# Larger recurrence steps, and TensorE in written order, in the first stage of a hybrid decoder layer

## The chip, the cores and the metric

The kernel runs on one core of one Trainium2 chip. Its time is the device time of one execution in microseconds (us); a run of a kernel is summarised by the median of its executions. Profiles come from one profiled execution.

Five engines work side by side, each through its own instructions in order: TensorE (PE in the profile; its weight loads are PEld), VectorE (DVE), ScalarE (ACT), GpSimd (POOL) and SyncE (SP), which here issues nearly all DMA transfers. They wait for each other by semaphores.

## What is computed

One layer on 2048 tokens of width 1024, all in float32:

```
h = RMSNorm(x)
[hgrn2 columns | rwkv7 columns] = h @ W_in           # 2048 + 1792 columns
o_hgrn2 = HGRN2 recurrence, 4 heads of 128           # S_t = diag(f_t) S_{t-1} + k_t v_t^T
o_rwkv7 = RWKV-7 recurrence, 8 heads of 64           # S_t = S_{t-1} diag(w_t) + (S_{t-1} a_t) b_t^T + v_t k_t^T
x = x + concat(o_hgrn2, o_rwkv7) @ W_out
x = x + ConvFFN(RMSNorm(x))                          # up, causal conv w=3, SiLU gate, down; d_ff 2816
out = RMSNorm(x)
```

## The kernel before

**Stages.** `phase1` (stage 1) computes the input projection, both recurrences and the output projection of three of the four token blocks of 512. Stage 2 does the last output projection, the up-projection, the convolution and gate, and the down-projection. The change is in stage 1 alone.

**Matmuls in three.** A projection in float32 is made of three matmuls on operands split in a high and a low part (`mm3`, lines 258 to 261): `hh*wh`, `hl*wh`, `hh*wl`. The weights are loaded as `wraw`, cast to `wh` on ACT (line 243) and subtracted to `wl` on DVE (line 244).

**Three streams.** Stage 1 is written as three Python generators, whose instructions are emitted in turn:

- `dense()` yields after each `mm3`, with a cost in ns (648 in a projection, 680 in an output projection). It goes through all projection columns, evicts each accumulator into `rkv`, `hq`, `hf`, `hv`, `hgg` and so on, transposes (`turn`, `transposed`) and runs `out_block`.
- `rw_super(nb, s_)` computes RWKV-7 for one block and two pairs of heads, a superblock; there are eight, one after the other.
- `hg_unit(nb, j)` computes HGRN2 for one block and one head; there are sixteen.

A loop at the end of `phase1` takes one step of `rw_super` (to its next `yield`), one of `hg_unit`, and then as many `mm3` of `dense` as make up `TICK` ns:

```python
        while any(alive.values()):
            for key, g in (("r", rw_), ("h", hg_)):
                ...
            fill(TICK)
```

With costs of 770 us in all, `TICK` 2000 gives about 386 rounds. The order so written is a priority: the Tile framework's scheduler, which works when the program is built, then puts each engine's instructions into an order of its own, in which an instruction that it expects to wait is passed by others. At run time each engine takes its instructions strictly in the built order.

**A superblock, in order.** Line numbers are those of before.

1. `ai`: two pairs of matmuls with the decay and gate LoRA weights (627, 629), sigmoids, a scan on DVE (637), exponentials; `W` is set to 1 in a column (643).
2. Norms through matmuls with `blk1` (648, 666); products `RT`, `AT`, `KB`, `BV` on DVE (649 to 676).
3. `M`: 64x128 matmuls (687), masked by DVE multiplies (690).
4. The 32x32 diagonal blocks of `M` go to DRAM (`Ed`, 703) and come back with one block per partition (`E`, 705).
5. Transposes `KBT`, `AT`, `v` (711 to 725), `lv` (742).
6. `Ti`, set to the identity (750, 751), becomes the inverse in 31 row steps of a multiply and an add on DVE (757, 759), with a yield after every fourth.
7. `Ti` and its transposed copy `TiT` (764) go to DRAM (`Td`, 763, 765) and come back as `TZ` (775) and `TTs` (772).
8. `z` (786), `z2` (800), `qu` (814), `yg` (834), `xp` and `yp` (850, 857) are small matmuls, each followed by an eviction.
9. `ch`: eight serial steps (868), each with a DVE multiply; then `yp` (878), a norm (886), the gate `gm` (898) and the output.

**A unit of HGRN2.** `scaled(l)` makes four DVE multiplies per level (927 to 932) for seven levels on `q`, `k`, `f` and `Sf`, which starts as ones (920). The levels' matmuls are at 948, transposes at 990, the state at 1001 and the output at 1010 and 1011.

Pool buffers of DRAM, SBUF and PSUM are few in stage 1: two PSUM banks for projections (`pj`), two for HGRN2 (`hg`), two double banks for RWKV-7 (`rw`), and four `wraw`.

Of the kernel before, what the change touches and what calls it, by code (L numbers as in the profile page):

```python
# [7 lines left out]
F32 = mybir.dt.float32  # L8
# [3 lines left out]
AF = mybir.ActivationFunctionType  # L12
# [6 lines left out]
P = 128  # L19
# [4 lines left out]
NBLK = T // BLK  # L24
FF = 2816
NFF = FF // P
TICK = 2000.0
NEG_C = -0.6065306597126334
HG_SCALE = 128.0 ** -0.5

# [31 lines left out]
def tile_layer(ctx, tc, consts, x, norm1_w, w_in, hg_lb_logits, hg_norm_w, rw_shift_mu, rw_w0, rw_w2,  # L62
# [3 lines left out]
    nc = tc.nc  # L66
    V, S, TE = nc.vector, nc.scalar, nc.tensor
# [41 lines left out]
    def act(out_, in_, func, **kw):  # L109

        want = tables.get(func)
        if want is not None and want != tab["now"]:
            pre = S.preload_act_table_set(want)
            for u_ in tab["uses"]:
                tc.add_manual_dep(pre.ins, u_.ins.name, NOSYNC, reason="table order")
            tab.update(now=want, pre=pre, uses=[])
        i_ = S.activation(out_, in_, func, **kw)
        if want is not None:
            tc.add_manual_dep(i_.ins, tab["pre"].ins.name, NOSYNC, reason="table order")
            tab["uses"].append(i_)  # L120
        return i_
# [141 lines left out]
    def phase1(c1):  # L263
# [3 lines left out]
        rp = c1.enter_context(tc.tile_pool(name="rp", bufs=1, reuse_waits="tile"))  # L267
# [342 lines left out]
        def rw_super(nb, s_):  # L610
# [6 lines left out]
            def tile_(tag, shape, name):  # L617
                return rp.tile([P] + shape, F32, tag=tag, name=name)

            def bank2():  # L620
                return ps.tile([P, 2, BLK], F32, tag="rw", name="rw", bufs=2)

            ai = tile_("KBT", [2, 2, BLK], "ai")
            a, iW = ai[:, 0], ai[:, 1]
# [5 lines left out]
            for u in U:  # L630
                act(a[:, u], bs_[u][:, 0, :], AF.Sigmoid, bias=vec("a0", prs[u]))
                act(iW[:, u], bs_[u][:, 1, :], AF.Sigmoid, bias=vec("w0", prs[u]))
            yield
            mk_ = tile_("M", [4, 2, BLK], "mk")
            c, km, sq = mk_[:, 0], mk_[:, 1], mk_[:, 2]
            for u in U:
                V.tensor_tensor_scan(c[:, u], scanm, iW[:, u], 0.0, ALU.mult, ALU.add)
                act(sq[:, u], k[:, u], AF.Square, scale=vec("kk", prs[u]))
                act(km[:, u], a[:, u], AF.Identity, bias=oka[:, prs[u]:prs[u] + 1], scale=vec("ka", prs[u]))
            yield  # L640
            W = tile_("UV", [16, 65], "W")
            WC = tile_("WC", [16, 1], "WC")
            V.memset(W[:, :, 0:1], 1.0)
            act(W[:, :, 1:65], c16(c), AF.Exp, scale=NEG_C)
            act(iW, c, AF.Exp, scale=-NEG_C)
            b1 = bank2()
            for u in U:
                TE.matmul(b1[:, u, :], blk1, sq[:, u], start=True, stop=True)
            V.tensor_scalar_max(sq, b1, 1e-24)
            V.tensor_mul(km, km, k)  # L650
            yield
            act(sq, sq, AF.Ln)
            act(sq, sq, AF.Exp, scale=-0.5)
            V.tensor_copy(WC, W[:, :, 64:65])
# [11 lines left out]
                TE.matmul(b1[:, u, :], blk1, BV[:, u], start=True, stop=True)  # L666
            for u in U:
                V.scalar_tensor_tensor(c[:, u], k[:, u], vec("kk", prs[u]), sq[:, u], ALU.mult, ALU.mult)
            yield
            V.scalar_tensor_tensor(AT, r4(c), -1.0, W4[:, :, :, 0:64], ALU.mult, ALU.mult)  # L670
            KB = tile_("KB", [8, 4, 64], "KB")
            V.tensor_mul(KB[:, :, 0::3, :], v16(km), v16(iW))
            yield
            V.tensor_mul(a, a, iW)
            V.tensor_mul(KB[:, :, 1:3, :], v16(c), v16(a))
            V.tensor_mul(BV, b1, v)
# [3 lines left out]
            for j in range(2):  # L680
                for u in U:
                    s1 = bank2()
                    for i in range(4):
                        b, e = 2 * j + i // 2, i % 2
                        for h in range(2):
                            hr = slice(h * 64, h * 64 + 64)
                            TE.matmul(s1[:, h, i * P:i * P + P], KB[hr, 4 * u + b, 2 * e:2 * e + 2, :],
                                      AR[hr, u, :, 2 * b + e, :], start=True, stop=True)
                    for h in range(2):
                        V.tensor_mul(M[:, u, :, 2 * j:2 * j + 2, h, :].rearrange("p e b t -> p b e t"),  # L690
                                     s1[:, h].rearrange("p (b e t) -> p b e t", e=2, t=P),
                                     s1m.unsqueeze(1).unsqueeze(1).broadcast_to([P, 2, 2, P]))
                    yield

            E = rp.tile([P, 32, 32], F32, tag="E", name="E")
            Ed = dp.tile([64, 32, 32], F32, tag="Ed", name="Ed", bufs=2)
# [7 lines left out]
                            M[r0:r0 + 32, u, e, :, :, 32 * q:32 * q + 32].rearrange("p b h t -> p (b h) t"))  # L704
            dma(E[0:64], Ed)

            KBT = tile_("KBT", [2, 8, P], "KBT")
            for u in U:
                tp = bank2()
# [19 lines left out]
            act(RHS[64:128, :, :, 0:64], tpv[0:64], AF.Copy)  # L729
            act(RHS[0:64, :, :, 0:64], tpv[64:128], AF.Copy)  # L730
            done["rw1"] += 1
            yield

            lv = bank2()
            for u in U:
                for b in range(4):
                    for h in range(2):
                        for e in range(2):
# [4 lines left out]
                                      UV[kr:kr + 64, 4 * u + b, e, h * 64:h * 64 + 64], start=True, stop=True,  # L743
                                      tile_position=(kr, r0))
            act(RHS[:, :, :, 64:128], lv.rearrange("p u (b h t) -> p (u b) h t", h=2, t=64), AF.Copy)
            yield

            n = 64
            Ti = rp.tile([P, 32, 32], F32, tag="Ti", name="Ti")
            V.memset(Ti[0:n], 0.0)  # L750
            V.memset(Ti[0:n].rearrange("m a b -> m (a b)")[:, 0:1024:33], 1.0)
            yield
            for j in range(31):
                nr, ncol = 31 - j, j + 1
                tmp = rp.tile([P, 272], F32, tag="etmp", name="etmp")
                tv = tmp[0:n, 0:nr * ncol].rearrange("m (a b) -> m a b", b=ncol)
                V.tensor_mul(tv, E[0:n, j, j + 1:32].unsqueeze(2).broadcast_to([n, nr, ncol]),
                             Ti[0:n, j, 0:ncol].unsqueeze(1).broadcast_to([n, nr, ncol]))
                V.tensor_add(Ti[0:n, j + 1:32, 0:ncol], Ti[0:n, j + 1:32, 0:ncol], tv)
                if j % 4 == 3:  # L760
                    yield
            TiT = rp.tile([P, 32, 32], F32, tag="E", name="TiT")
            dma(Td[0], Ti[0:n])
            V.tensor_copy(TiT[0:n], Ti[0:n].rearrange("m a b -> m b a"))
            dma(Td[1], TiT[0:n])
            TZ = tile_("XH", [2, 2, 4, 2, 32], "TZ")
            for u in U:
                for e in range(2):
                    r0 = er0(e)
                    for q in range(2):  # L770
# [3 lines left out]
                    m0 = u * 32 + e * 16  # L774
                    dma(TZ[r0:r0 + 32, 0, u].rearrange("p b h t -> p (b h) t"),
                        Td[0, m0:m0 + 8].rearrange("m s t -> s m t"))
            for _ in range(2):
                yield
            z = bank2()
            for u in U:  # L780
                for b in range(4):
# [64 lines left out]
            for u in U:  # L846
                for ch in range(8):
                    b, e = ch // 2, ch % 2
# [4 lines left out]
            for u in U:  # L853
                for ch in range(8):
                    b, e = ch // 2, ch % 2
# [6 lines left out]
            for ch in range(8):  # L862
                b, e = ch // 2, ch % 2
# [42 lines left out]
        def hg_unit(nb, j):  # L906
# [6 lines left out]
            for b in range(4):  # L913
                TE.transpose(tp[:, b * P:(b + 1) * P], v[:, b * P:(b + 1) * P], ident)
            act(VT, tp.rearrange("p (b t) -> p b t", t=P), AF.Copy)
            yield
            A = rp.tile([P, 4, 64], F32, tag="hA", name="A")
            Pf = f
            Sf = rp.tile([P, BLK], F32, tag="Sf", name="Sf")
            V.memset(Sf, 1.0)  # L920

            def scaled(l):

# [34 lines left out]
            Xs = []  # L958
            for l in range(3):
                Xs.append(scaled(l))  # L960
                yield
            l0, l1 = bank("hg"), bank("hg")
            level(l0, 0, k, q)
            for l in range(3):
# [1 line left out]
            V.tensor_mul(A, l0[:, 0:256].rearrange("p (b t) -> p b t", t=64), dgm.unsqueeze(1).broadcast_to([P, 4, 64]))  # L966
            for l in range(3):
                take(l, l1, l * 128)
            yield
            Xs = []  # L970
            for l in range(3, 6):
                Xs.append(scaled(l))
                yield
            l1 = bank("hg")
            for l in range(3, 6):
                level(l1, (l - 3) * 128, Xs[l - 3], Xs[l - 3], l)
# [1 line left out]
                take(l, l1, (l - 3) * 128)  # L978
            act(Af[0:64, :, 0:64], A[0:64], AF.Copy)
            act(Af[64:128, :, 64:128], A[64:128], AF.Copy)  # L980
            yield
            X = scaled(6)
            V.tensor_mul(k, k, Sf)
            V.tensor_mul(q, q, Pf)
# [71 lines left out]
        while any(alive.values()):  # L1056
            for key, g in (("r", rw_), ("h", hg_)):
                if alive[key]:
                    try:
                        next(g)  # L1060
                    except StopIteration:
                        alive[key] = False
            fill(TICK)


    if "1" in stages:
        with ExitStack() as c1:
            phase1(c1)
    cx.close()

# [13 lines left out]
    with ExitStack() as c2:  # L1084
# [35 lines left out]
        with tc.tile_pool(name="op", bufs=1, reuse_waits="tile") as op_:  # L1120
# [4 lines left out]
            b = NBLK - 1  # L1125
# [363 lines left out]
```

## Time and profile before

| | |
|---|---|
| median of 3 runs | 2780.48 us (2779.83 to 2783.94) |
| span of the profiled execution | 2783.2 us |
| last projection matmul of stage 1 starts | 1416.33 us |
| first matmul of stage 2 starts | 1425.53 us |
| input-projection matmuls into `pj`, three lines of 960 | 401.8 + 379.9 + 379.0 us busy |
| DMA | 435.01 MB, mean 156 GB/s |

A row of a timeline reads: start in us, duration, engine, line, operation, output<-inputs, shapes, count, and in brackets the idle time before it with what ended it. "SPq" is a DMA issue on SP. A row of a group of instructions ends with their busy time in us and the mean in ns, then the idle time before them. A row of waits reads: engine, output and line, what it waited for, total us, times, longest. A row of windows gives the stretch, its length, then for PE, PEld, DVE, ACT and POOL the busy us with the number of instructions, then the granted share of the TensorE clock, the share of the DMA engines and GB/s; "sum" adds up the stretches asked for. A matmul's duration includes its way through the array; matmuls overlap, so the distance from start to start is what one occupies.

### The profile page before, as it was taken

The page shows a single profiled execution, that of the slowest core. Times are in us where ns is not written, and L with a number is a line of the kernel's source. Part 1 is how long each engine was busy: PE and PEld are TensorE (multiplying, and loading weights), DVE is VectorE, ACT ScalarE, POOL GpSimd, SP SyncE. Part 2 cuts the span into 40 slices and gives each one's busy share as a digit, 9 for nine tenths or more (in the row PEclk, how much of TensorE's full clock was granted, in tenths as well). Part 3 has the DMA queues.
Part 4 walks back from the last instruction along what each step waited for, and adds up shares of the span by engine and source line. Part 5 has one row for each costly group of instructions (what it writes and reads, how often), then busy time and mean ns, then how long its engine had stood idle before and what let it go on. Part 6 is the DMA issues. An engine that isn't in the chain of part 4 may idle for free.

```text
span 2783.2 us, 47784 instructions
## 1 busy us (share of the span) xinstructions
PE 2678.8 (96%) x18059; PEld 2135.2 (77%) x18059; DVE 2066.4 (74%) x3877; ACT 1421.1 (51%) x2254; POOL 11.1 (0%) x24
## 2 busy tenths in 40 slices
PE   8999999989999999999989999998999999999998
PEld 6877777767787777777767888886888888877887
DVE  4867778685686766868658789989997877677656
ACT  5445454544646446435346765456455555445444
POOL 0000000000000000000000000000000000000000
PEclk9999999999999999999899999999999999999999
DMA  5222322244441344543475457756672223998855
GB/s 163 72 69 72 99 73 78 63 131 141 131 121 58 102 141 136 161 132 94 131 239 178 143 172 262 239 165 216 205 245 88 87 76 135 324 333 310 289 193 186
DMA packets 429628, 435.01 MB, mean 156 GB/s; under 512 B 68703, under 2 KB 288213, under 8 KB 429397
## 3 DMA queue, kind: packets, MB, share of 16 engines
q1 hardware_dynamic: 428337, 429.30, 48.4%
q8 instruction: 142, 2.33, 0.3%
q0 software_dynamic: 992, 2.64, 0.2%
q14 instruction: 89, 0.73, 0.1%
q10 hardware_dynamic: 68, 0.02, 0.0%
HBM read 325.94 MB, written 105.91 MB: 155 GB/s over the span
## 4 chain that ended last, share of the span: by engine, by line
PE 78%; DVE 7%; ACT 7%; DMA 4%; issue 3%; SPq 1%; DVEq 0%; ACTq 0%
PE pj L259 8%; PE pj L260 8%; PE pj L261 8%; PE ua L261 6%; PE ua L259 5%; PE ua L260 5%; PE ud L259 3%; PE ud L260 3%; PE ud L261 3%; PE da L260 2%; PE da L261 2%; PE da L259 2%; PE hg L948 2%; PE db L259 2%; PE db L260 2%
## 5 line engine op out<-in xcount | busy, mean ns | idle before, releaser
L259 PE MATMUL pj<-hh,wh 128*128 128x512 f32 x960 | 401.8, 419 | 0.9 <-DVE xh L398 0.4
L260 PE MATMUL pj<-hl,wh 128*128 128x512 f32 x960 | 379.9, 396 | 0.0
L261 PE MATMUL pj<-hh,wl 128*128 128x512 f32 x960 | 379.0, 395 | 0.2 <-DVE wl L244 0.2
L243 ACT CAST wh<-wraw 128x512 fp32r<-128x512 f32 x240 | 147.0, 619 | 307.9 <-PE pj L260 266.2
L259 PE MATMUL ua<-Bh,uwh 128*128 128x512 f32 x704 | 278.6, 396 | 15.0 <-ACT uwh L243 13.7
L261 PE MATMUL ua<-Bh,uwl 128*128 128x512 f32 x704 | 276.6, 393 | 0.7 <-DVE uwl L244 0.7
L260 PE MATMUL ua<-Bl,uwh 128*128 128x512 f32 x704 | 276.5, 393 | 0.0
L244 DVE TENSOR_TENSOR wl<-wraw,wh 128x512 fp32r<-128x512 f32 x240 | 163.3, 686 | 133.8 <-ACT wh L243 132.9
L259 PEld LDWEIGHTS pj<-hh,wh 128*128 128x128 f32 x960 | 180.8, 188 | 53.1 <-issue 13.6
L260 PEld LDWEIGHTS pj<-hl,wh 128*128 128x128 f32 x960 | 180.9, 188 | 42.4 <-issue 7.9
L243 ACT CAST uwh<-uraw 128x512 fp32r<-128x512 f32 x220 | 134.9, 618 | 151.2 <-PE ua L260 80.0
L261 PEld LDWEIGHTS pj<-hh,wl 128*128 128x128 f32 x960 | 180.7, 188 | 39.9 <-issue 1.3
L243 ACT CAST dah<-draw 128x512 fp32r<-128x512 f32 x151 | 93.8, 621 | 182.7 <-PE da L260 50.5
L244 DVE TENSOR_TENSOR uwl<-uraw,uwh 128x512 fp32r<-128x512 f32 x220 | 146.9, 685 | 50.8 <-ACT uwh L243 50.8
L244 DVE TENSOR_TENSOR dal<-draw,dah 128x512 fp32r<-128x512 f32 x151 | 104.2, 690 | 107.0 <-ACT dah L243 106.8
L259 PEld LDWEIGHTS ua<-Bh,uwh 128*128 128x128 f32 x704 | 133.5, 190 | 44.0 <-ACT uwh L243 14.3
L261 PEld LDWEIGHTS ua<-Bh,uwl 128*128 128x128 f32 x704 | 133.6, 190 | 30.4 <-DVE uwl L244 2.3
L260 PEld LDWEIGHTS ua<-Bl,uwh 128*128 128x128 f32 x704 | 133.6, 190 | 27.2
L259 PE MATMUL ud<-Bh,uwh 128*128 128x512 f32 x352 | 137.9, 392 | 1.9 <-DVE cv L1340 1.9
L261 PE MATMUL ud<-Bh,uwl 128*128 128x512 f32 x352 | 137.1, 389 | 0.0
L260 PE MATMUL ud<-Bl,uwh 128*128 128x512 f32 x352 | 137.0, 389 | 0.0
L260 PE MATMUL da<-dbl,dah 128*128 128x512 f32 x340 | 133.5, 393 | 1.7 <-DVE dbl L244 1.6
(314 smaller groups left out, 5959.7 us busy)
## 6 DMA issues: line engine op xcount, KB each, us to landing
wraw<-in_w_in_dram SPq DMA_DIRECT2D x240, 256.0 KB, 3.0
uraw<-in_w_up_dram SPq DMA_DIRECT2D x176, 256.0 KB, 3.3
woraw<-in_w_out_dram SPq DMA_DIRECT2D x96, 256.0 KB, 3.1
draw<-Sg SPq DMA_DIRECT2D x88, 256.0 KB, 2.9
draw<-Tw SPq DMA_DIRECT2D x88, 256.0 KB, 3.0
gd<-y SPq DMA_DIRECT2D x86, 256.0 KB, 2.9
xt<-x1d SPq DMA_DIRECT2D x32, 512.0 KB, 6.6
draw<-gd SPq DMA_DIRECT2D x63, 256.0 KB, 5.1
```

The source lines that it names most:

```text
L243: S.copy(hi, src)
L244: V.tensor_sub(lo, src, hi.bitcast(F32))
L259: TE.matmul(acc, lh, rh, start=first, stop=False, skip_group_check=skip)
L260: TE.matmul(acc, lh, rl, start=False, stop=False, skip_group_check=skip)
L261: TE.matmul(acc, ll, rh, start=False, stop=last, skip_group_check=skip)
L948: TE.matmul(o, kt[:, t0:t0 + 64], qs, start=True, stop=True, tile_position=(0, e * 64))
```

## The change

- `TICK` goes from 2000 to 3250, and yields are taken out of `rw_super` and `hg_unit`, so that each step holds more. The loop makes 243 rounds.
- The scheduler is told to leave PE's instructions of `phase1` in the order in which they are written. Other engines are scheduled as before.
- The inverse becomes a generator of four parts (rows 0 to 7, 8 to 15, 16 to 23, 24 to 30). The first part is written just ahead of the yield before `lv`, the second after `lv`; two more steps hold the others. `Ti`'s memsets move up to behind the `E` load. One yield instead of two separates the `Td` transfers from `z`.
- The memsets of `W`, `Ti` and `Sf` go from DVE to POOL, and the copy `TiT` from DVE to ACT.

```diff
-TICK = 2000.0
+TICK = 3250.0
...
-            V.memset(W[:, :, 0:1], 1.0)
+            nc.gpsimd.memset(W[:, :, 0:1], 1.0)
...
-                    yield
+                yield
...
+            n = 64
+            Ti = rp.tile([P, 32, 32], F32, tag="Ti", name="Ti")
+            nc.gpsimd.memset(Ti[0:n], 0.0)
+            nc.gpsimd.memset(Ti[0:n].rearrange("m a b -> m (a b)")[:, 0:1024:33], 1.0)
+
+            def rows_of(js):
+                for j in js:
+                    nr, ncol = 31 - j, j + 1
+                    tmp = rp.tile([P, 272], F32, tag="etmp", name="etmp")
+                    tv = tmp[0:n, 0:nr * ncol].rearrange("m (a b) -> m a b", b=ncol)
+                    V.tensor_mul(tv, E[0:n, j, j + 1:32].unsqueeze(2).broadcast_to([n, nr, ncol]),
+                                 Ti[0:n, j, 0:ncol].unsqueeze(1).broadcast_to([n, nr, ncol]))
+                    V.tensor_add(Ti[0:n, j + 1:32, 0:ncol], Ti[0:n, j + 1:32, 0:ncol], tv)
+
+            def inverse_in(parts):
+                for a_, b_ in parts:
+                    rows_of(range(a_, b_))
+                    yield
+
+            inverse = inverse_in(((0, 8), (8, 16), (16, 24), (24, 31)))
...
             done["rw1"] += 1
+            next(inverse)
             yield
...
             act(RHS[:, :, :, 64:128], lv.rearrange("p u (b h t) -> p (u b) h t", h=2, t=64), AF.Copy)
-            yield
-
-            n = 64
...
-                if j % 4 == 3:
-                    yield
+            next(inverse)
+            yield
+            for _ in inverse:
+                yield
             TiT = rp.tile([P, 32, 32], F32, tag="E", name="TiT")
             dma(Td[0], Ti[0:n])
-            V.tensor_copy(TiT[0:n], Ti[0:n].rearrange("m a b -> m b a"))
+            act(TiT[0:n], Ti[0:n].rearrange("m a b -> m b a"), AF.Copy)
...
-            for _ in range(2):
-                yield
+            yield
             z = bank2()
...
-            V.memset(Sf, 1.0)
+            nc.gpsimd.memset(Sf, 1.0)
...
             for l in range(3):
                 Xs.append(scaled(l))
-                yield
+            yield
...
-        with ExitStack() as c1:
+        with ExitStack() as c1, tc.manual_schedule(engines={mybir.EngineType.PE}):
             phase1(c1)
```

Left out are the other removed yields: four in the first part of `rw_super`, and in `hg_unit` those after `VT`, after the first levels, inside the second three levels and after `Af`.

More of the change, by code (lines that the diff above doesn't have):

```diff
@@ L692, in rw_super @@
                                      s1m.unsqueeze(1).unsqueeze(1).broadcast_to([P, 2, 2, P]))
-                    yield
+                yield
             E = rp.tile([P, 32, 32], F32, tag="E", name="E")
@@ L745, in rw_super @@
             act(RHS[:, :, :, 64:128], lv.rearrange("p u (b h t) -> p (u b) h t", h=2, t=64), AF.Copy)
+            next(inverse)
             yield
-            n = 64
[L749 to L759, printed above, removed]
-                if j % 4 == 3:
-                    yield
+            for _ in inverse:
+                yield
             TiT = rp.tile([P, 32, 32], F32, tag="E", name="TiT")
             dma(Td[0], Ti[0:n])
-            V.tensor_copy(TiT[0:n], Ti[0:n].rearrange("m a b -> m b a"))
+            act(TiT[0:n], Ti[0:n].rearrange("m a b -> m b a"), AF.Copy)
             dma(Td[1], TiT[0:n])
@@ L776, in rw_super @@
                         Td[0, m0:m0 + 8].rearrange("m s t -> s m t"))
-            for _ in range(2):
-                yield
+            yield
             z = bank2()
@@ L915, in hg_unit @@
             act(VT, tp.rearrange("p (b t) -> p b t", t=P), AF.Copy)
-            yield
             A = rp.tile([P, 4, 64], F32, tag="hA", name="A")
@@ L960, in hg_unit @@
                 Xs.append(scaled(l))
-                yield
+            yield
             l0, l1 = bank("hg"), bank("hg")
@@ L968, in hg_unit @@
                 take(l, l1, l * 128)
-            yield
             Xs = []
@@ L972, in hg_unit @@
                 Xs.append(scaled(l))
-                yield
+            yield
             l1 = bank("hg")
@@ L980, in hg_unit @@
             act(Af[64:128, :, 64:128], A[64:128], AF.Copy)
-            yield
             X = scaled(6)
```

## Prediction

> **What bounds the kernel now.** I began with the page, then asked for the sums of stage 1 (the part that the change touches, up to its last projection matmul), then for the chain that ends in line 786's `z` matmuls.
>
> ```profile
> span 2783.2 us, 47784 instructions
> PE 2678.8 (96%) x18059; PEld 2135.2 (77%) x18059; DVE 2066.4 (74%) x3877; ACT 1421.1 (51%) x2254; POOL 11.1 (0%) x24
> ```
> ```profile
> 0.00:1416.30 1416.30, 1351.48 (x12256) 1049.32 (x12257) 1007.11 (x2280) 704.38 (x1111) 9.28 (x21) 0.98 0.37 109
> ```
> TensorE is the bound: in stage 1 it is busy 1351 of 1416 us (columns: PE, PEld, DVE, ACT, POOL, clock). Only 65 us are idle, 11 of them the start; so little can be won there and much lost. VectorE at 1007 us (71%) has no such margin where its work bunches.
>
> ```profile
> PE pj L259 <- ACT wh L243: 7.7, 10, 1.7
> PE hg L990 <- DVE hk L983: 6.8, 3, 2.9
> PE pj L427 <- ACT xt L117: 4.9, 6, 1.3
> ```
> These are the largest waits beside the start: total, times, longest. None concerns `z`, although `z` ends the longest dependent chain. Eight times, once per RWKV superblock, the chain is: last `M` multiply on DVE, `Ed`/`E` through DRAM, 31 row steps of the 32x32 inverse, `Td` through DRAM, `z`. Its first occurrence, on DVE, SP and PE:
>
> ```profile
> 94.60 1.29 DVE L690 TENSOR_TENSOR M<-rw,cst 128x512 f32<-128x512 f32 x2 [0.61 <-PE rw L687]
> ...
> 102.93 0.18 DVE L757 TENSOR_TENSOR etmp<-E,Ti 64x31 f32<-64x31 f32 x1 [1.37 <-DMA E<-Ed]
> 103.14 0.20 DVE L759 TENSOR_TENSOR Ti<-Ti,etmp 64x31 f32<-64x31 f32 x1
> ...
> 142.68 0.18 DVE L759 TENSOR_TENSOR Ti<-Ti,etmp 64x31 f32<-64x31 f32 x1
> ```
> ```profile
> 142.89 0.47 SPq L763 DMA_DIRECT2D Td<-Ti  x1
> ...
> 145.80 0.91 SPq L775 DMA_DIRECT2D TZ<-Td  x2
> ...
> 151.53 0.45 SPq L775 DMA_DIRECT2D TZ<-Td  x1
> ```
> ```profile
> 149.74 0.24 PE L786 MATMUL rw<-TZ,M 32*32 32x32 f32 x2
> ```
> 55 us pass from 94.3 (last `M` matmul) to `z`. TensorE does not wait, because the scheduler put 168 projection matmuls in between. Over all eight such stretches (first row, and the sum):
>
> ```profile
> 94.30:149.70 55.40, 55.30 (x436) 46.00 (x432) 45.69 (x126) 25.83 (x39) 0.00 (x0) 1.00 0.33 83
> ...
> sum 494.80, PE 479.29 PEld 387.77 DVE 412.89 ACT 222.71 POOL 1.12; mean PE 59.91 PEld 48.47 DVE 51.61 ACT 27.84 POOL 0.14
> ```
> Inside them, from the first inverse row to the last:
>
> ```profile
> sum 334.30, PE 321.94 PEld 259.92 DVE 317.17 ACT 145.04 POOL 1.12; mean PE 40.24 PEld 32.49 DVE 39.65 ACT 18.13 POOL 0.14
> ```
> DVE is 95% busy there: the inverse is VectorE-bound, and TensorE is kept busy with borrowed projections.
>
> **The change, part by part.** I counted on the built order of both programs, which holds no times. The instructions are the same 13,915 matmuls. Stretches of projection and of other matmuls alternate 447 times instead of 622, so the change does what it says; that rival is closed.
>
> *Fewer visits.* What one visit costs:
>
> ```profile
> 1395.49 0.39 PE L260 MATMUL pj<-wl,hh 128*128 128x512 f32 x1
> 1395.72 0.39 PE L261 MATMUL pj<-wh,hl 128*128 128x512 f32 x1
> 1396.04 0.45 PE L868 MATMUL rw<-XH,M 64*64 64x64 f32 x8
> 1396.41 0.50 PE L259 MATMUL pj<-wh,hh 128*128 128x512 f32 x1
> 1396.75 0.39 PE L260 MATMUL pj<-wl,hh 128*128 128x512 f32 x1
> ```
> Projections follow each other every 0.23 us. The one before the visit takes 0.32, the first one after it 0.34, and the visit's own last matmul holds the array about 0.12 longer: 0.09 + 0.11 + 0.12 = 0.32 us. 622 - 447 = 175 switches are 87 visits: 87 x 0.32 = 28 us saved (0 if TensorE waits at those places anyway).
>
> *The inverse, started earlier but with less to cover it.* In written order TensorE does nothing past `z` until `TZ` lands. Cover: between `M` and `z` the new order has 105, 105, 105, 99, 87, 105, 87 and 102 projections, 795 in all, against 1408 before. Those 1408 took 1408 x 0.227 = 320 of the 495 us; the other 175 us held 1408 small matmuls (a coincidence), 0.124 each with their visits. The new stretches hold 1228 small ones: 795 x 0.227 + 1228 x 0.124 = 180 + 153 = 333 us of cover. Pricing each small kind by its own spacing gives 311, the lower bound.
>
> Chain: the `M` multiply 1.3 us; to the first inverse row 102.93 - 95.89 = 7.0; after the last row (142.9) the last `TZ` load is issued at 151.5 and `z` needs its landing, 10.6 with the 1.9 us that these loads take in the median:
>
> ```profile
> DMA to landing us min/median/max: 1.7/1.9/3.2
> ```
> The inverse's own 62 instructions, 0.29 us apart, are 18 us; in the windows above 426 other DVE instructions took 334 - 143 = 191 us, 0.45 each. The new order queues 309 others between first and last row: 143 + 309 x 0.45 = 282 us. Chain: 8 x (1.3 + 7.0 + 10.6) + 282 = 433 us. Against 333 that is 100 us of waiting, with 311 it is 122. Low bound: only the first `z` pair waits, 6.8 instead of 10.6, 70 us. High bound: `E` comes later, since the new SP order has other transfers between `Ed` and `E` in all eight, ten in one; 12 us instead of 7 adds 40, so 160. I take 110. Behind `z` on TensorE wait all later projections, and with them their evictions and the freeing of weight buffers. The z path is no longer covered by `ch`, the eight serial steps, which get 15 projections each where they need few.
>
> *Engines relieved.* Memsets and the `TiT` copy leave DVE:
>
> ```profile
> L764 DVE COPY TiT<-Ti 64x1024 f32<-64x1024 f32 x8 | 8.6, 1076 | 0.1
> L920 DVE MEMSET Sf<- 128x512 f32 x16 | 7.8, 485 | 0.9
> L750 DVE MEMSET Ti<- 64x1024 f32 x8 | 7.3, 912 | 1.3 <-issue 1.1 <-DMA wraw<-in_w_in_dram 0.2
> ```
> That is 24 us (under 2 more for the two small memsets). The queue just counted is without them, so this counts nothing again. On POOL the nearest row is as fast; ACT's nearest copy equals the 1.08 us:
>
> ```profile
> 18.92 0.60 POOL L281 MEMSET Af<- 128x512 f32 x1
> ```
> ```profile
> L117 ACT ACTIVATE KBT<-rw 128x1024 f32<-128x1024 f32 x16 | 15.7, 1022 | 11.2 <-PE rw L711 11.2
> ```
> Both are hidden by POOL's and ACT's slack; without it, up to 1 us per superblock.
> The Trainium skill, GPSIMD Engine Reference, section Specifications, speaks against the move: GpSimd shares SBUF interfaces with VectorE, in contention with instructions of two SBUF inputs. No row here shows it; by it up to these 24 us would return to DVE.
>
> *Start of a superblock.* Three steps instead of seven lead from `ai` to `M`.
>
> ```profile
> 65.42 2.38 DVE L637 TENSOR_TENSOR_SCAN mk<-cst,ai 128x512 f32<-128x512 f32 x2 [1.16 <-ACT ai L117]
> ...
> 82.38 1.22 DVE L675 TENSOR_TENSOR KB<-mk,ai 128x1024 f32<-128x1024 f32 x1
> ```
> From scan to the last `KB` DVE needs 18.2 us here, with 21 instructions; the new order has 16 to 21 (34 once), about 16 us. The cover, 45 projections (10.2) and some 6 us of other matmuls, is as long. I take +8, between 0 and 30.
>
> *HGRN2 steps.* Three levels of four DVE multiplies now come in one step; one level takes 1.6 us with its neighbours:
>
> ```profile
> 84.46 0.42 DVE L927 TENSOR_TENSOR hX<-hq,hf 128x256 f32<-128x256 f32 x1
> ...
> 86.05 1.28 DVE L690 TENSOR_TENSOR M<-rw,cst 128x512 f32<-128x512 f32 x2
> ```
> 4.8 us against 15 x 0.23 = 3.4 of projections plus the other stream's matmuls: 32 places, up to 1.9 us each, 60 us; where the other stream is long, nothing. I take 10.
>
> *Clock.* A short stop already halves it:
>
> ```profile
> 626.00:629.00 3.00, 0.40 (x4) 0.42 (x4) 2.97 (x8) 0.83 (x2) 0.00 (x0) 1.00 0.81 252
> 629.00:640.00 11.00, 11.00 (x129) 9.14 (x126) 3.42 (x11) 4.46 (x8) 0.00 (x0) 0.53 0.16 49
> 1349.00:1352.00 3.00, 0.17 (x6) 0.06 (x3) 2.96 (x10) 0.83 (x2) 0.00 (x0) 0.58 0.55 167
> 1352.00:1370.00 18.00, 17.88 (x164) 14.48 (x166) 5.76 (x13) 5.66 (x11) 0.00 (x0) 0.50 0.20 62
> ```
> After about 3 us of waiting, 10 to 18 us run at half clock: 5 to 9 us lost. Eight waits of 14 us would lose 40 at 5 each; 15 of that stand in these rows of before already: +25, bounds 0 and 60.
> The Trainium skill, TensorE: Matmul & The Clock Gate, Part 1, has the clock halve after one idle window of about 3.4 us and recover after one busy window. The 3 us stop agrees roughly, the 18 us recovery does not; by the rule the eight would lose 8 x 1.7 = 14 instead of 40, and the sum would be 26 lower.
>
> *Removed waits.* Of the 54 us idle after the start, the waits for splits shrink, since these catch up while TensorE waits at `z`; those round the transposes stay. -15, between 0 and -45.
>
> *Tail.* The last chain steps now follow the last projection.
>
> ```profile
> 1401.79 2.08 PE L878 MATMUL rw<-AR,XH 64*64 64x64 f32 x64
> ...
> 1410.63 1.98 PE L898 MATMUL rw<-gdt,g 128*128 128x512 f32 x4 [0.55 <-ACT yo L117]
> ...
> 1425.53 0.79 PE L259 MATMUL wacc<-woh,Bh 128*128 128x512 f32 x1 [8.81 <-ACT Bh L236]
> ```
> L878 to the end of L898 is 10.8 us, where 8.8 idle before stage 2 today: +2 (0 to 3).
>
> **Sum:** -28 + 110 + 8 + 10 + 25 - 15 + 2 = +112; 2783.2 + 112 = 2895. The median run, 2780.5, lies 2.7 below the profiled span: 2892 us.
>
> **The rivals.** (1) *Faster.* The inverse's queue shortens below the cover. Decision point: 433 must fall to 333, that is 12.5 us per superblock, or 28 fewer others in each queue of 25 to 45. For it: DVE loses 25 us and the first 16 rows stand ahead of `lv`. Against it: in-order DVE cannot skip what is queued. Then -28, and a good third of the 54 us idle, -20: 2735 us.
> (2) *Much slower.* HGRN2's levels wait as well, and the repeated stops keep the clock low: 60 and 60 instead of 10 and 25, `E` late: +40. Sum +237, 3017 us. For it: the 1349 row, where the clock was low before the stop ended. Against it: `ch` has time to spare.
> (3) *No change*: savings and waits cancel; it needs the low bounds throughout: -28 + 70 - 45 = -3.
>
> **How the numbers follow.** Forecast 0.70 (own range 2815 to 2985), faster 0.18 (2700 to 2775), much slower 0.08 (2985 to 3070), no change 0.04. All bounds at once would give 2777 to 3065; the range 2745 to 2995 takes in the low end and a part of the faster case, and leaves out the rest of that and the slowest times, together about 0.19. A measurement tells 0.2%, 5.6 us, from no change: faster 0.18, same 0.03, slower 0.79 (the no-change case spills a little to the slower side).
>
> **What would show it.** Right: idle TensorE before `z` with a DMA or `TZ` as releaser, 8 times, 8 to 20 us; half clock behind each; DVE over 90% busy there; shorter total of projection spacing elsewhere. Wrong: `z` without a wait, or stage 1 ending before 1416; then the inverse queue ran faster than its count, or cover was longer than priced.

## The result, and the profile after

| | before | after |
|---|---|---|
| median of 4 runs | 2780.15 us (2779.82 to 2783.94) | 2951.07 us (2950.55 to 2953.0) |
| ratio to before, 95% interval | | 1.0608 (1.0588 to 1.0627) |
| span of the profiled execution | 2783.2 us | 2951.2 us |
| last projection matmul of stage 1 | 1416.3 us | 1575.1 us |
| TensorE idle up to there | 64.8 us | 218.3 us |

The kernel became 6% slower, 59 us beyond the forecast of 2892 and inside the stated range of 2745 to 2995. The page of after, its first lines and the row of the granted clock:

```profile
span 2951.2 us, 47846 instructions
...
PE 2692.2 (91%) x18059; PEld 2150.7 (73%) x18059; DVE 2054.6 (70%) x3829; ACT 1459.3 (49%) x2280; POOL 29.1 (1%) x64
...
PEclk9899899998998989979999999999999999999999
```

TensorE does the same 18059 matmuls in nearly the same busy time; what grew is the time in which it does nothing. The dents of the clock row lie in the first 21 of 40 slices, which is stage 1. The windows of stage 1 of after (busy us of PE, PEld, DVE, ACT, POOL, then clock, DMA share, GB/s):

```profile
0.00:1575.10 1575.10, 1356.80 (x12168) 1062.42 (x12169) 992.33 (x2227) 739.14 (x1131) 27.30 (x61) 0.93 0.34 98
```

Of the 168.0 us that the span grew, 158.8 fall before stage 1's last projection: 153.5 are idle TensorE (64.8 to 218.3), 5.3 are busy (1351.5 to 1356.8). Another 3.8 lie between that matmul and stage 2, and 5.4 after it. The waits of TensorE in stage 1 of after (total us, times, longest):

```profile
PE rw L790 <- DMA TZ<-Td: 104.1, 24, 16.8
PE hg L951 <- DVE hX L931: 18.9, 12, 2.0
PE rw L683 <- DVE KB L671: 15.5, 6, 4.0
PE pj L260 <- DVE wl L244: 14.1, 17, 5.8
PE pj L259 <- ACT wh L243: 12.0, 9, 4.3
...
PE pj L259 <- DVE hgg L357: 7.2, 2, 4.7
```

The first row is the predicted wait: line 790 is `z`. Its pieces add up to between 1.5 and 21.4 us in one superblock. Before had no such row, and its largest wait beside the start was 7.7 us. The chain of the first superblock, as the timelines of after show it on DVE, SP and PE, to be laid beside the same stretch of before:

```profile
93.90 1.28 DVE L686 TENSOR_TENSOR M<-rw,cst 128x512 f32<-128x512 f32 x2
...
102.67 0.18 DVE L713 TENSOR_TENSOR etmp<-E,Ti 64x31 f32<-64x31 f32 x1 [1.78 <-DMA E<-Ed]
...
137.10 0.18 DVE L715 TENSOR_TENSOR Ti<-Ti,etmp 64x31 f32<-64x31 f32 x1
```
```profile
137.35 0.48 SPq L768 DMA_DIRECT2D Td<-Ti  x1
...
139.28 0.46 SPq L770 DMA_DIRECT2D Td<-TiT  x1
140.24 0.85 SPq L780 DMA_DIRECT2D TZ<-Td  x2
```
```profile
136.15 0.39 PE L261 MATMUL pj<-hh,wl 128*128 128x512 f32 x1
...
142.41 1.22 PE L790 MATMUL rw<-TZ,M 32*32 32x32 f32 x32 [5.87 <-DMA TZ<-Td]
...
147.01 0.31 PE L790 MATMUL rw<-TZ,M 32*32 32x32 f32 x2 [3.38 <-DMA TZ<-Td]
...
148.40 1.06 PE L790 MATMUL rw<-TZ,M 32*32 32x32 f32 x30 [1.08 <-DMA TZ<-Td]
```

The inverse ends at 137.1, 5.6 us sooner than before. But TensorE had run out of projections at 136.5 and stood, in three pieces, until the last of the four `TZ` loads had landed at 148.4. The stretches from the last `M` matmul to the first `z` (the first of eight, and their sum), then from the first inverse row to the last (sum):

```profile
92.00:142.40 50.40, 39.60 (x343) 32.64 (x339) 38.14 (x111) 17.99 (x25) 1.09 (x2) 0.92 0.28 70
...
sum 451.80, PE 330.09 PEld 270.72 DVE 348.11 ACT 193.53 POOL 10.86; mean PE 41.26 PEld 33.84 DVE 43.51 ACT 24.19 POOL 1.36
```
```profile
sum 293.90, PE 219.91 PEld 178.70 DVE 274.41 ACT 123.72 POOL 2.67; mean PE 27.49 PEld 22.34 DVE 34.30 ACT 15.46 POOL 0.33
```

The eight stretches became 43 us shorter (494.8 to 451.8), yet TensorE idles 121.7 us in them (451.8 - 330.1) instead of 15.5. DVE stays 93% busy while the inverse runs (274.4 of 293.9). The clock around two of the stops, in windows of after:

```profile
136.00:143.00 7.00, 1.13 (x21) 0.71 (x21) 1.15 (x6) 1.94 (x1) 1.09 (x2) 0.85 0.62 145
143.00:155.00 12.00, 7.54 (x72) 6.45 (x69) 2.23 (x6) 2.39 (x4) 0.53 (x1) 0.52 0.19 30
318.00:335.00 17.00, 0.79 (x5) 0.32 (x4) 12.89 (x39) 3.79 (x3) 1.09 (x2) 0.61 0.73 221
335.00:346.00 11.00, 5.81 (x72) 4.71 (x73) 0.01 (x1) 1.81 (x4) 0.00 (x0) 0.52 0.20 31
```

The clock is halved while TensorE waits, and the 12 and 11 us behind the wait, filled with `z` and its followers, run at half speed too.

### The profile page after: what moved, and what is told of

Its sections match the earlier page's. It is cut to its first block, busy times and chain, and to the rows that moved or that the text cites. A ratio compares the mean times of both kernels' runs of the same rounds, so it can differ in the third digit from the quotient of the medians.

```text
span 2951.2 us, 47846 instructions
## 1 busy us (share of the span) xinstructions
PE 2692.2 (91%) x18059; PEld 2150.7 (73%) x18059; DVE 2054.6 (70%) x3829; ACT 1459.3 (49%) x2280; POOL 29.1 (1%) x64
## 4 chain that ended last, share of the span: by engine, by line
PE 67%; DVE 13%; DMA 9%; ACT 6%; issue 3%; SPq 2%; ACTq 0%; DVEq 0%
PE pj L259 7%; PE pj L260 7%; PE pj L261 6%; PE ua L259 5%; PE ua L261 5%; PE ua L260 5%; PE ud L259 2%; PE ud L260 2%; PE ud L261 2%; PE da L260 2%; PE da L261 2%; PE da L259 2%; PE hg L951 1%; DVE wl L244 1%; DVE Ti L715 1%
## 5 line engine op out<-in xcount | busy, mean ns | idle before, releaser
L259 PE MATMUL pj<-hh,wh 128*128 128x512 f32 x960 | 415.8, 433 | 7.9 <-ACT xt L117 6.9
L259 PEld LDWEIGHTS pj<-hh,wh 128*128 128x128 f32 x960 | 186.2, 194 | 61.7 <-issue 12.4
L243 ACT CAST uwh<-uraw 128x512 fp32r<-128x512 f32 x220 | 134.4, 617 | 143.4 <-PE ua L260 70.7
L259 PE MATMUL ud<-Bh,uwh 128*128 128x512 f32 x352 | 137.9, 392 | 2.3 <-DVE cv L1341 2.3
L261 PE MATMUL ud<-Bh,uwl 128*128 128x512 f32 x352 | 137.1, 389 | 0.0
L260 PE MATMUL ud<-Bl,uwh 128*128 128x512 f32 x352 | 137.1, 389 | 0.0
```

The lines of the kernel that those rows point to most:

```text
L243: S.copy(hi, src)
L259: TE.matmul(acc, lh, rh, start=first, stop=False, skip_group_check=skip)
L260: TE.matmul(acc, lh, rl, start=False, stop=False, skip_group_check=skip)
L261: TE.matmul(acc, ll, rh, start=False, stop=last, skip_group_check=skip)
```

## The experiments

Two theories stood at the start. *Cover*: in written order TensorE cannot pass `z`, and too few projections stand between `M` and `z` to outlast the chain through the inverse; all else is small. Its rival, *steps*: the larger steps themselves, with their bunched DVE and ACT work, starve TensorE wherever they fall. Ratios are to before, with 95% intervals, each from runs on one chip. Idle time and time at half clock, where no row is quoted, are added up from the traces over stage 1; in before they are 64.8 and 54.6 us, in after 218.3 and 221.9. Where an expectation speaks of 133 us of waiting at `z`, it counts 28.8 us twice: the row of 104.1 us holds those between `z`'s own matmuls already.

**The two halves of the change, each alone.** In the first, after without the written order:

```diff
-        with ExitStack() as c1, tc.manual_schedule(engines={mybir.EngineType.PE}):
+        with ExitStack() as c1:
```

> The changed kernel with TensorE's stage 1 given back to the scheduler; steps, inverse in parts and relieved engines stay. Theory (the loss is TensorE standing at z in written order): the built order has 1172 projections between M and z instead of 795, so the wait at z falls from 133 us to under 20 us, and the time to 2780 to 2820 us. Rival (the larger, bunched steps themselves overload VectorE): the time stays above 2880 us.

Measured: 2814.59 us, ratio 1.0102 (1.0078 to 1.0125). Idle 82.8 us, half clock 71.7 us. Two of its waits:

```profile
PE hg L991 <- DVE hk L984: 10.4, 6, 2.6
...
PE hg L951 <- DVE hX L931: 7.2, 7, 1.8
```

`z` waits for `TZ` for 1.2 us in all: the scheduler put 1172 projections between `M` and `z`, against 795 in written order. It also put small stretches back, with 585 alternations instead of 447, so the visits that the larger steps saved mostly returned. Without the written order, the rest of the change, of which the larger steps are a part, costs 1%.

In the second, before with the written order:

```diff
-        with ExitStack() as c1:
+        with ExitStack() as c1, tc.manual_schedule(engines={mybir.EngineType.PE}):
```

> The kernel before with TensorE in written order and nothing else changed (386 rounds). Theory: the written order has 1026 projections between M and z, against 1408 as scheduled and 795 in the changed kernel; 382 x 0.227 = 87 us less cover than before, so 50 to 90 us of waits at z and some 20 us of clock: 2850 to 2900 us, between the two kernels. Rival (written order costs nothing, the step sizes do): 2780 to 2800 us.

Measured: 2912.49 us, ratio 1.0464 (1.0438 to 1.049), 12 us more than the expected 2900 at most. Idle 183.6 us, half clock 204.8 us. Its largest waits:

```profile
PE rw L786 <- DMA TZ<-Td: 96.2, 27, 11.9
PE pj L260 <- DVE wl L244: 14.2, 16, 2.8
```

With the old 386 rounds the same wait for `TZ` appears, 96 us, although 1026 projections stand before `z`. So the written order does the harm with either size of step. In parts of before's time: 1.0% for the change without the order, 4.6% for the order alone, 6.1% for both.

**Without the chain's rows.** After with the 31 row steps left out, so that `Ti` stays the identity and its 164 us of DVE work are missing:

```diff
-                for j in js:
+                for j in ():
```

> The changed kernel without the 31 row steps of the inverse (the inverse stays the identity). Theory: the chain from M to z loses its 294 us on VectorE, all waiting at z goes (133 us) and with it a part of the half clock (25 us), and VectorE is relieved elsewhere: 2760 to 2810 us. Rival (stops are spread over all in-order places): over 2870 us.

Measured: 2785.02 us, ratio 1.0005 (0.9993 to 1.0016). Idle 90.9 us, half clock 61.4 us; DVE is busy 856.8 us in stage 1. Three of its waits:

```profile
PE rw L683 <- DVE KB L671: 17.0, 6, 4.0
...
PE pj L259 <- ACT wh L243: 11.2, 10, 2.5
...
PE hg L951 <- DVE hX L930: 3.3, 5, 1.3
```

The wait for `TZ` is gone, and with it all that the change lost. On balance, written order and larger steps then cost nothing that can be measured; before without its rows, the nearest comparison, was not run. The edit also takes load off DVE, so this run alone does not tell the chain from that load. The run without the written order does: there DVE has all its work, and 1% is lost. The waits that are left are the small ones.

**Cover moved to where it lacks.** After, with the same projections dealt out otherwise: 2.4 times as many in each of the four rounds between `lv` and `z`, 0.3 times in the eight `ch` rounds.

```diff
             next(inverse)
-            yield
+            yield 2.4
             for _ in inverse:
-                yield
+                yield 2.4
...
-            yield
+            yield 2.4
             z = bank2()
...
-                yield
+                yield 0.3
...
-            fill(TICK)
+            fill(TICK * share)
```

> The changed kernel with the same rounds, but the four rounds ahead of z hold 2.4 times the projections and the eight serial ch rounds 0.3 times: 1458 projections between M and z instead of 795, which adds 663 x 0.227 = 150 us of cover. Theory: waits at z fall from 133 us to under 15 us, half clock in stage 1 from 222 us to under 120, time 2790 to 2830 us. Rival (the inverse only takes longer, since VectorE has the splits of more projections in the same stretch; or ch now stalls): over 2880 us.

Measured: 2864.74 us, ratio 1.0284 (1.0261 to 1.0307): half of the loss is gone, less than expected. Idle 144.8 us, half clock 112.6 us. Its waits:

```profile
PE pj L259 <- ACT wh L243: 29.3, 19, 5.4
PE rw L790 <- DMA TZ<-Td: 23.5, 9, 7.3
PE pj L260 <- DVE wl L244: 17.5, 28, 3.4
PE rw L683 <- DVE KB L671: 17.1, 6, 4.0
```

The wait for `TZ` fell from 104.1 to 23.5 us, as the theory of cover says. But 663 more projections in these stretches need their weights split there, and `wh` and `wl` now keep TensorE waiting for 46.8 us instead of 26.1. The inverse takes as long as before this edit (292.8 us from first rows to last, summed, against 293.9), but `z` now comes 137.9 us after its end instead of 53.5: more cover than needed, with waits inside it. Only 4.8 of the 46.8 us fall between the first and the last row of an inverse; 26.2 fall between the last row and `z`, where DVE has no rows left. Of the 29.3 us for `wh`, 14.6 end with an ACT that had itself waited for the load of an output-projection weight. The longest of them, on PE and ACT:

```profile
1032.37 0.80 PE L259 MATMUL pj<-wh,hh 128*128 128x512 f32 x1 [5.36 <-ACT wh L243]
```
```profile
1031.69 0.62 ACT L243 CAST wh<-woraw 128x512 fp32r<-128x512 f32 x1 [4.00 <-DMA woraw<-in_w_out_dram]
```

Another 10 us are lost between the last projection and stage 2: 19.5 us here, 9.2 in before.

**The subtractions on another engine.** The run with moved cover, and with `wl`'s subtractions on GpSimd, meant to take them out of the inverse's way:

```diff
-        V.tensor_sub(lo, src, hi.bitcast(F32))
+        (nc.gpsimd if name == "w" else V).tensor_sub(lo, src, hi.bitcast(F32))
```

> The kernel of e5_cover with the 240 subtractions that make wl on POOL instead of VectorE. Theory (what is left there is projections that wait for their splits behind the inverse in VectorE's order): waits on wh and wl fall from 47 us to under 15, the inverse's windows from 293 to about 255 us, time 2810 to 2835 us. Rival (GpSimd is slow or holds up VectorE): waits on wl grow and the time is 2870 us or more.

Measured: 2933.82 us, ratio 1.0537 (1.0523 to 1.0551), much worse than the run without this edit. `wl` and `wh` still keep TensorE waiting for 45.6 us, where under 15 were expected. Groups of this run (busy us, mean ns, idle before), below them the same two DVE groups of after:

```profile
L244 POOL TENSOR_TENSOR wl<-wraw,wh 128x512 fp32r<-128x512 f32 x240 | 346.1, 1445 | 787.4 <-ACT wh L243 755.2 <-PE pj L260 15.5 <-ACT nst L117 7.4
...
L715 DVE TENSOR_TENSOR Ti<-Ti,etmp 64x31 f32<-64x31 f32 (+15 forms) x248 | 124.7, 503 | 5.5
...
L933 DVE TENSOR_TENSOR Sf<-Sf,hf 128x256 f32<-128x256 f32 x112 | 61.0, 545 | 0.7
```
```profile
L715 DVE TENSOR_TENSOR Ti<-Ti,etmp 64x31 f32<-64x31 f32 (+15 forms) x248 | 82.1, 331 | 3.4
...
L933 DVE TENSOR_TENSOR Sf<-Sf,hf 128x256 f32<-128x256 f32 x112 | 47.0, 420 | 0.5
```

The subtraction takes 1445 ns on GpSimd in the mean and 687 on DVE, and while it runs there DVE's own instructions with two tensor inputs slow down: 331 to 503 ns in the inverse's adds, 420 to 545 in HGRN2. The inverse, which the move was to free, takes 308.8 us from first rows to last instead of 292.8. Sorted by whether a subtraction ran on GpSimd meanwhile, the 128x256 multiplies of lines 933 and 935 take 915 and 1026 ns beside one and 421 and 422 otherwise; line 300, which reads one of its inputs from PSUM, takes 749 and 740. This is what the Trainium skill says in GPSIMD Engine Reference, section Specifications: the two engines contend for SBUF where DVE's instruction has two SBUF inputs. The rows agree, and give the size. How much of the 69 us by which this run is slower than the one before it comes from that was not separated.

**Stops filled with idle work.** After with 40 matmuls of 128x512 in front of each `z`, written to a half of its PSUM tile that is not in use; they add nothing but activity.

```diff
             z = bank2()
+            for _ in range(40):
+                TE.matmul(z[:, 1, :], hh[:, 0, 0:P], hh[:, 0, :], start=True, stop=True)
```

> The changed kernel with 40 extra 128x512 matmuls ahead of each z, on operands that are there already, into a half of z's PSUM tile that nothing reads: 9 us of TensorE work in each of the eight waits. Theory (the waits cost twice, once as idle and again as half clock behind them, some 39 us more than before): waits at z shrink by about 70 us because they are filled, half clock falls by 60 us or more and the time falls by 15 to 30 us, to 2920 to 2935 us, although work was added. Rival (the clock plays no part in the loss): 2950 us or more.

Measured: 2951.82 us, ratio 1.0609 (1.0593 to 1.0625), the same as after, where 15 to 30 us less were expected. The wait:

```profile
PE rw L792 <- DMA TZ<-Td: 42.3, 18, 8.6
```

Idle time fell by 61.0 us (218.3 to 157.3) and half clock from 221.9 to 143.4 us. But the 320 matmuls lengthen the written order by 320 x 0.2265 = 72.5 us, 11.5 more than the idle time that they replaced, so in some superblocks they probably outran the wait, which now comes in 18 pieces instead of 24. Time lost to half clock, half of what TensorE ran at it, fell by 11 us, from 63.5 to 52.1. The two cancel. The run does not settle what the clock alone costs: the counted 38 us more than before (25.4 to 63.5) is an upper reading.

**The relieved engines alone.** Before with the memsets on GpSimd and `TiT` on ACT:

```diff
-            V.tensor_copy(TiT[0:n], Ti[0:n].rearrange("m a b -> m b a"))
+            act(TiT[0:n], Ti[0:n].rearrange("m a b -> m b a"), AF.Copy)
...
-            V.memset(Sf, 1.0)
+            nc.gpsimd.memset(Sf, 1.0)
```

> The kernel before with the memsets of W, Ti and Sf on POOL and the TiT copy on ACT alone. Theory: VectorE loses 25 us, TensorE stays the bound: between -10 and 0 us against before (2770 to 2780). Rival (GpSimd memsets hold up VectorE's two-input instructions): slower than before, with longer mean times of the DVE rows.

Measured: 2787.94 us, ratio 1.0015 (1.0005 to 1.0026), a small loss where none or a gain was expected. Two groups of this run:

```profile
L117 ACT ACTIVATE TiT<-Ti 64x1024 f32<-64x1024 f32 x8 | 16.8, 2104 | 2.2 <-DVE Ti L759 2.2
...
L930 DVE TENSOR_TENSOR Sf<-Sf,hf 128x256 f32<-128x256 f32 x112 | 47.1, 421 | 0.6
```

DVE's busy time in stage 1 falls by 18.6 us, but the copy takes 2104 ns on ACT instead of 1076 on DVE, in the middle of the chain. `Sf` stays at 421 ns (418 before), and the two of its 112 multiplies that ran beside a memset took 418. What makes the loss of 0.15% is not shown.

**The early inverse with the old rounds and the scheduler.** Before with these edits and with the inverse written early, in eight parts:

```diff
+            inverse = inverse_in(((0, 4), (4, 8), (8, 12), (12, 16), (16, 20), (20, 24), (24, 28), (28, 31)))
...
+            next(inverse)
             yield
...
-            V.memset(Ti[0:n], 0.0)
...
-                if j % 4 == 3:
-                    yield
+            for _ in inverse:
+                yield
```

> The kernel before (386 rounds, scheduler) with the relieved engines and the inverse written ahead of lv in eight parts. Theory: the scheduler covers z either way, so within 10 us of before; the 31 us by which the scheduled kernel with 243 rounds lies above before come from the larger rounds. Rival (the early inverse crowds VectorE): 2795 to 2815 us like that kernel.

Measured: 2794.25 us, ratio 1.0034 (1.0022 to 1.0046), which lies at the border of the two expectations. With the runs above this lays out the 1.0% that the change costs under the scheduler: 0.15% for the relieved engines, 0.2% for the early inverse, and by difference 0.7% for the larger rounds (with the inverse in four parts for eight). The runs come from two chips, and each of these parts is uncertain by 0.1 to 0.3%. Which wait of the larger rounds makes these 0.7% was not separated further.

**The four loads that `z` needs, first.** In the code of both kernels, the eight `TTs` loads and the `TiT` copy are written among and ahead of the four `TZ` loads. After, with the order turned round and `TiT` back on DVE:

```diff
-            TiT = rp.tile([P, 32, 32], F32, tag="E", name="TiT")
             dma(Td[0], Ti[0:n])
-            act(TiT[0:n], Ti[0:n].rearrange("m a b -> m b a"), AF.Copy)
-            dma(Td[1], TiT[0:n])
             TZ = tile_("XH", [2, 2, 4, 2, 32], "TZ")
             for u in U:
                 for e in range(2):
                     r0 = er0(e)
+                    m0 = u * 32 + e * 16
+                    dma(TZ[r0:r0 + 32, 0, u].rearrange("p b h t -> p (b h) t"),
+                        Td[0, m0:m0 + 8].rearrange("m s t -> s m t"))
+            TiT = rp.tile([P, 32, 32], F32, tag="E", name="TiT")
+            V.tensor_copy(TiT[0:n], Ti[0:n].rearrange("m a b -> m b a"))
+            dma(Td[1], TiT[0:n])
```

> The changed kernel with the four TZ loads issued ahead of the eight TTs loads, and TiT back on VectorE. Theory (the end of the chain, Td through DRAM to the last TZ, is on the path in full): the second wait inside z (28.8 us in all) goes, and 0.9 us for each TiT, since the ACT copy takes 1.99 us and the VectorE copy 1.08; 25 to 40 us with the clock, 2910 to 2927 us. Rival (z2 then waits for TTs instead, or the queue does): 2940 us or more.

Measured: 2916.44 us, ratio 1.0494 (1.0478 to 1.051). The wait, 10 pieces in place of 24:

```profile
PE rw L793 <- DMA TZ<-Td: 72.0, 10, 16.0
```

32 us less waiting, and 1.1% of before's time less, which is 32 us too. The same edit on the run with moved cover:

> The kernel of e5_cover with the same two edits. Theory: its waits on TZ (23.5 us) nearly go, those on splits (47 us) stay: 2835 to 2855 us. Rival (the over-long cover hides the chain already, the splits are all): 2860 to 2870 us.

Measured: 2850.36 us, ratio 1.0253 (1.0238 to 1.0268). Its waits:

```profile
PE pj L259 <- ACT wh L243: 27.3, 21, 4.0
...
PE pj L260 <- DVE wl L244: 15.6, 25, 3.4
...
PE rw L793 <- DMA TZ<-Td: 10.5, 2, 6.0
```

Little of the wait for `TZ` is left, and the 42.9 us for splits remain. And the same edit on before:

> The kernel before with the four TZ loads ahead of the TTs loads. Theory: the scheduler covers this chain already, so no difference beyond what another built order makes: 2775 to 2790 us. Rival (z's end matters there too): under 2770 us.

Measured: 2780.43 us, ratio 1.0005 (0.9996 to 1.0014). There the chain is covered, and a shorter one is worth nothing. No version was found that beats before.

## Why the prediction was right, and where its sizes were off

*The place and the mechanism* were right: TensorE waits at `z` for `TZ` in all eight superblocks, for 8.5 to 21.4 us in seven of them and 1.5 in the fourth; the clock is halved in and behind those seven waits, and DVE is over 90% busy while the inverse runs. Taking the rows out of the chain removes the whole loss; letting the scheduler pass `z` removes five sixths of it. The rival of larger steps holds for the sixth that is left at most.

*Cover, 333 us*: TensorE is busy 330.1 us in the eight stretches. (The prediction's counts of small matmuls, 1408 and 1228, were each 64 too high; with 1344 and 1164 its sum changes by under 2 us.)

*Chain, 433 us*: it was 480, and this is the first term that was mis-sized. By its parts, predicted and measured over eight superblocks:

| | predicted | before | after |
|---|---|---|---|
| last `M` matmul to last `M` multiply | 10 | 16 | 18 |
| to the first inverse row | 56 | 78 | 86 |
| first row to last | 282 | 334 | 294 |
| to the last `z` load in use | 85 | | 82 |

The last figure is 53.5 us to the first `z` plus 28.8 of waiting inside it. The second row is the error: 7.0 us was read from the first superblock and multiplied by eight, though the trace of before had it at 9.8 in the mean. The windows of before and after for it (the shortest and longest of eight, and the sum):

```profile
914.00:920.30 6.30, 6.30 (x43) 5.53 (x42) 2.05 (x3) 3.07 (x5) 0.00 (x0) 1.00 0.42 104
1128.70:1141.60 12.90, 12.10 (x126) 10.12 (x125) 3.38 (x6) 8.68 (x11) 0.00 (x0) 1.00 0.86 222
...
sum 78.00, PE 77.07 PEld 67.94 DVE 23.22 ACT 50.59 POOL 0.00; mean PE 9.63 PEld 8.49 DVE 2.90 ACT 6.32 POOL 0.00
```
```profile
95.20:102.70 7.50, 7.50 (x51) 6.65 (x50) 3.07 (x8) 4.20 (x6) 0.00 (x0) 1.00 0.50 110
...
840.20:855.80 15.60, 14.71 (x112) 11.99 (x113) 3.36 (x7) 12.15 (x16) 0.00 (x0) 1.00 0.82 233
...
sum 86.10, PE 79.34 PEld 67.48 DVE 42.35 ACT 46.35 POOL 0.07; mean PE 9.92 PEld 8.44 DVE 5.29 ACT 5.79 POOL 0.01
```

The longest are those with the highest DMA share, 0.86 and 0.82; but in before 12.4 us also came at a share of 0.27, so the share alone does not explain them. That other transfers stand between `Ed` and `E` was put into the high bound only (12 us each); 10.8 came.

*Waiting at z, +110*: 480 - 330 = 150 us of idle TensorE in the stretches and inside `z`, against 22.4 before. So +128, between the value taken and the high bound of 160. That 110 lies so near is in part luck: the chain was 47 us too short, but the 22.4 us of before were not taken off either. The row of `z` holds 104 of the 150. The rest TensorE meets on its way there, mostly (38 us) at instructions that wait for DVE while the inverse fills it; where it waits for those, it waits the less at `z`.

*Removed waits, -15*: this had the wrong sign. The waits for `wl` and `wh` grew from 2.9 and 7.7 us to 14.1 and 12.0, and `hgg` brought 7.2. Of these 26.1 us of splits 11.8, and all of `hgg`, fall between the first and the last row of an inverse, where DVE is 93% busy and what is queued behind its rows is late. Why the other 14.3 did not shrink was not followed up.

*Start of a superblock, +8*: idle between `ai` and `M` went from 13.0 to 36.4 us, +23, with 15.5 of it at `KB`; within its bounds. *HGRN2 levels, +10*: 18.9 us at line 951, also within bounds, but not a term of its own: every one of these waits falls between the first and the last row of an inverse, so that they are a part of the 150 us. Without the rows line 951 waits 3.3 us. (The high bound of 60 us does not follow from its own rows: 4.8 - 3.4 is 1.4 us a place, 45 for 32 places.)

*Visits, -28, and clock, +25*: TensorE's busy time rose by 5.3 us in all. The time lost at half clock, by counting, went from 25.4 to 63.5 us, +38 instead of +25, which leaves -33 for the visits and all else. Their sum is measured, the split between them only counted. The Trainium skill (TensorE: Matmul & The Clock Gate, Part 1) has one busy window of about 3.4 us bring the clock back. The smaller loss that the prediction worked out by it, 14 us instead of 40, lies further from what came. The 12 us at 0.52 from 143 to 155 us do not speak against it, since TensorE was busy for 7.54 of them only; what made the loss larger is that such a window came late, behind the whole of `z`. The rows of before at 629 and 1352 us, at half clock with TensorE busy 11.00 of 11.00 and 17.88 of 18.00 us, do not fit it.

*Engines relieved, 0*: the ACT row chosen for `TiT`, an equally large copy without a transposed read, was the wrong neighbour. In after the copy takes 1987 ns:

```profile
L117 ACT ACTIVATE TiT<-Ti 64x1024 f32<-64x1024 f32 x8 | 15.9, 1987 | 34.7 <-DVE Ti L715 34.7
```

On POOL the memsets were no burden, though 0.60 us for 128x512 was not quite "as fast" as DVE's 0.485. The copy costs 0.9 us more per superblock, 7 us, near the bound of 1 us each that the prediction gave, and part of the 82 us in the table. *Tail, +2*: 3.8 us.

Together the idle terms were forecast at 110 + 8 + 10 - 15 = 113 us and came to 153.5 (128 at `z` and on the way to it, 23 at the starts, 2 elsewhere). The difference of 40.5, the clock's 13.1 and 7.2 us behind the last projection of stage 1 (3.8 and 5.4 came for the tail's 2), less 4.8 us that the visits saved beyond their 28, make up the 56 us by which the sum of 112 fell short of 168.

## What to carry to other kernels

Before an in-order engine is held to the written order, add up for every long dependent chain what is written between its two ends on that engine, and compare it with the chain's length over all its occurrences, not the first one. Cover has to be fed: 663 projections moved into the chain's stretch took 81 us off the wait at its end and added 21 us of waits for their split weights, and the loss was only halved. An edit that is worth nothing while a chain is covered, as the four `TZ` loads put first, can be worth some 30 us once the cover is gone (there with `TiT` back on VectorE).

## What the hardware did that was not expected

- A copy of 64x1024 floats with a transposed read took 1987 to 2104 ns on ACT, where DVE took 1076 and where ACT copied 128x1024 floats from PSUM without the transposition in 1022. Which of the differences costs the time was not separated.
- Subtractions of 128x512 on GpSimd slowed DVE's instructions with two inputs in SBUF by 30 to 52% (420 to 545 and 331 to 503 ns), averaged over all of them; those of lines 933 and 935 that ran beside one took over twice their time (915 and 1026 ns, otherwise 421 and 422). The two `Sf` multiplies beside a memset were not slowed (418 ns). But one DVE copy of 128x128 beside a GpSimd memset took 940 ns in before, where the other 15 took 221 in the mean.
- Half clock outlasts the stop: 143 to 155 us at 0.52, of which TensorE was busy 7.54, and 335 to 346 us at 0.52, busy 5.81. Behind the seven long waits at `z` it ended each time with the first 3.4 us, the step of the clock's record, that TensorE filled without a gap. In before 11 us from 629 us on ran at 0.53 although TensorE was busy throughout, with 129 matmuls, nearly all small. So a full TensorE is not always enough; what is was not found out.
